# A decoder trunk on one NeuronCore: its opening written in another order, with the first norm folded

## The chip, the cores and the metric

The kernel runs on one core of one Trainium2 chip. Its time is the device time of one launch in microseconds (us): 993.72 us is the median of three runs (992.82 to 994.13). One execution was profiled; it took 992.12 us, of which its span, from the first instruction to the last, is 990.1 us. In what follows PE is TensorE, PEld its weight loads, DVE is VectorE, ACT is ScalarE, POOL is GpSimd and SP is SyncE, which here only issues transfers.

## The reference

A trunk of two layers over 1024 positions of 1024 channels, f32. Only the first sub-layer matters here:

```
c_act = silu(c)
shift, scale, gate = split(c_act @ ada_w[0] + ada_b[0], 3)
h = (x * rsqrt(mean(x*x, -1) + eps) * norm_g[0]) * (1 + scale) + shift
u, z = split(h @ a_w_in, 2);  p = causal_multiscale_pool(u)      # four groups of 512 channels
y = grouped(p) @ a_w_group * a_scale;  x = x + gate * ((y * silu(z)) @ a_w_out)
```

After it come a shared K/V, a sliding-window attention layer with sinks, and a final norm. In group 0 the kernel multiplies the input weight by the group weight first ("joined" weight), so that the pooled product needs one matmul chain less.

## The kernel before, in words

Channels lie on partitions, positions on the free axis; position halves of 512 are called q = 0 and 1, and the eight blocks of 128 channels k = 0 to 7. A float32 product is made of three passes in the faster fp32r format: each operand is split in a rounded part "h" and a rest "l" (`h` by ACT, `l = raw - h` by DVE or POOL), and h*h, h*l and l*h are summed in PSUM.

The opening, which ends at the first matmul of the gates (L218), is a list of calls (L424 to L550) under a manual schedule: on each of the five engines the instructions stand in just the order in which they are written, and each engine takes them in that order. What it does:

- SP issues loads in the order of L425 to L434: four chunks `ci` of the two weights to be joined (`wgr`, `raw`, 0.25 and 0.5 MiB), the halves of `x` (0.25 MiB each), then the scale tiles `ad` (two of 0.5 MiB for each k, L294). The buffers of `raw` and of `ad` are two each, so later loads wait until the earlier content is used.
- `split_wg` and `split_wu` (L299, L304) split a chunk; `join_mm` (L312) makes 96 matmuls of 512 columns, 8 output blocks by 4 chunks by 3 passes; `joined_h` and `joined_l` split the joined weight w0 again (for blocks 2, 3, 6 and 7 ACT copies it and POOL subtracts, L329 and L336).
- c, one row, is spread to 128 partitions by a matmul with ones (L459, here as two fp32r passes of `crow`), then silu is made of it (`cact`, L468 and L470).
- `square2` and `add2` (L407, L416) make the sum of squares of x over the eight blocks, `rstd_stats` (L136) sums it over partitions with 1-column matmuls and takes the power -0.5 on POOL, `rstd_spread` (L154) spreads it to a tile `rbs[q]`.
- `dots(k, i)` (L342) gives shift (i = 0) and scale (i = 1) of block k: a DVE product-and-sum over 1024 columns (L247), after which `mod_scale` (L266) makes the column `acol`.
- For each k and q, `first_xn` (DVE, x times rstd, L181), `first_h` (ACT makes h, L163, and again the same in f32, L378; POOL makes l, L379), and `first_mm` (12 matmuls, L402) with w0. For k = 0 the f32 value and l are made by DVE (`soon_h`, `soon_l`).

`first_mm` runs for k = 0, 4, 1, 5, 2, 6, 3, 7. After the opening `block_sums` (L607) forms sums and differences of the modulated blocks for the gates' and inputs' products. From there on the instructions keep the order that the kernel before has.

Of the kernel before, what the change touches and what calls it, by code (L numbers as in the profile page):

```python
# [49 lines left out]
CONST_FILL = 56  # L50
# [5 lines left out]
def trunk(ctx, tc, xT, c, pack, ada_first, ada_rest, wu0_in, wg0_in, wa, wg, wao, wkv,  # L56
# [57 lines left out]
    acol = cp.tile([P, 24], F32, name="acol")  # L114
# [107 lines left out]
    with ExitStack() as sa:  # L222
# [19 lines left out]
        crow = hp.tile([P, 2, T], F32R, tag="h", name="crow")  # L242
        onesr = sp.tile([P, H], F32R, tag="xn", name="onesr", bufs=5)[:, :P]
        nc.vector.tensor_copy(out=onesr[0:1, :], in_=ones[0:1, :].broadcast_to([1, P]))

# [81 lines left out]
        copies = {}  # L327

        def joined_raw(*ms):  # L329

            for m in ms:
                if m % 2 == 0:
                    copies[m // 2] = tmp()
                nc.scalar.copy(out=copies[m // 2][:, half(m % 2)], in_=jb[m])

        def joined_sub(*ms):  # L336
            for m in ms:
                w = w0[m // 2][:, m % 2]
                nc.gpsimd.tensor_sub(out=w[:, 1, :], in0=copies[m // 2][:, half(m % 2)],
                                     in1=w[:, 0, :].bitcast(F32))  # L340
# [6 lines left out]
        xns = {}  # L347

        def first_xn(k, q):
            xns[k, q] = xn_tile(k, q, rbs[q])  # L350
# [30 lines left out]
        def soon_h(k, q):  # L381
            a, b, h, _ = first_parts(k, q)
            mod_h(xns[k, q], a, b, h)
            nc.vector.tensor_scalar(out=first_f(k, q), in0=xns[k, q], scalar1=a, scalar2=b,
                                    op0=ALU.mult, op1=ALU.add)

        def soon_l(k, q):
            _, _, h, l = first_parts(k, q)
            nc.vector.tensor_sub(out=l, in0=first_f(k, q), in1=h.bitcast(F32))
# [14 lines left out]

        sqs = {}

        def square2(n, q):  # L407

            if n < 2:
                sqs[n, q] = sq2[q][n]  # L410
            elif n % 2 == 0:
                t = tmp()
                sqs[n, q], sqs[n + 1, q] = t[:, half(0)], t[:, half(1)]
            nc.scalar.activation(sqs[n, q], xk[n][:, half(q)], AF.Square)

        def add2(n, q, eng=None):  # L416
            s = sq2[q][n % 2]
            (eng or nc.vector).tensor_add(out=s, in0=s, in1=sqs[n, q])

        def fold(q):  # L420
            nc.vector.tensor_add(out=sq2[q][0], in0=sq2[q][0], in1=sq2[q][1])

        ET = mybir.EngineType
        with tc.manual_schedule(engines={ET.PE, ET.Activation, ET.DVE, ET.Pool, ET.SP}):  # L424
            fetch_c(0, (half(0), half(1)))  # L425
            nc.sync.dma_start(pk, pack)
            fetch_c(1)
            fetch_x(0, range(4))
            fetch_c(2)
            fetch_c(3)  # L430
            fetch_x(0, range(4, 8))
            fetch_x(1, range(8))
            fetch_ada(0)
# [11 lines left out]

            warm(5)
# [3 lines left out]
            for cols in (half(0), half(1)):  # L450
                split_wu(0, cols)
            nc.vector.tensor_copy(out=crow[0:1, 0, :], in_=cact[0:1, :])
            nc.vector.tensor_sub(out=crow[0:1, 1, :], in0=cact[0:1, :],
                                 in1=crow[0:1, 0, :].bitcast(F32))
            for i in range(3):
                join_all(0, s=(i,))
            for q in range(2):
                for i in range(2):
                    mm(cbs[q], onesr[0:1, :], crow[0:1, i, half(q)], start=i == 0, stop=i == 1)  # L459
# [7 lines left out]
            for q in range(2):  # L467
                nc.scalar.activation(cact[:, half(q)], cbs[q], AF.Tanh, scale=0.5)  # L468
            for q in range(2):
                nc.vector.scalar_tensor_tensor(out=cact[:, half(q)], in0=cact[:, half(q)],  # L470
                                               scalar=1.0, in1=cbs[q], op0=ALU.add, op1=ALU.mult)
            split_wg(2)
            split_wu(2)
            join_all(2)
            split_wg(3)
            split_wu(3)
            nc.vector.tensor_scalar_mul(out=asch, in0=pk[:, C_ASC:C_ASC + 16], scalar1=0.5)
            nc.vector.tensor_scalar_mul(out=nsink, in0=pk[:, C_SINK:C_SINK + 16], scalar1=-1.0)
            for k in range(4, 8):
                square2(k, 0)  # L480
                add2(k, 0)
            fold(0)
            for k in range(3):
                square2(k, 1)
            join_all(3, (4, 5))
            rs = rstd_stats(sq2[0][0], 4)
            joined_h(4, 5)
            joined_l(4, 5)
            square2(3, 1)
            join_all(3, (0,))  # L490
            add2(2, 1)
            add2(3, 1, nc.gpsimd)
            square2(4, 1)
            joined_h(0)
            join_all(3, (1,))
            bc = rstd_spread(rs, 4)
            square2(5, 1)
            joined_l(0)
            joined_h(1)
            add2(4, 1)  # L500
            add2(5, 1, nc.gpsimd)
            nc.scalar.copy(out=rbs[0], in_=bc)
            join_all(3, (2, 3))
            square2(6, 1)
            joined_l(1)
            square2(7, 1)
            dots(0, 0)
            add2(6, 1, nc.gpsimd)
            joined_h(2, 3)
            joined_raw(2, 3)  # L510
            dots(0, 1)
            add2(7, 1)
            fold(1)
            joined_sub(2)
# [3 lines left out]
            for ci in range(3):  # L518
                join_mm(7, jb[7], ci)
            first_xn(0, 0)  # L520
            soon_h(0, 0)
            rs = rstd_stats(sq2[1][0], 4)
            soon_l(0, 0)
            joined_h(6)
            joined_raw(6)
            joined_sub(3)
            dots(4, 0)
            dots(4, 1)
            join_mm(7, jb[7], 3)
            bc = rstd_spread(rs, 4)  # L530
            first_mm(0, 0)
# [920 lines left out]
```

## Time and profile before

| | |
|---|---|
| median of three runs | 993.72 us |
| the profiled execution | 992.12 us |
| its span | 990.1 us |
| PE busy | 964.8 us (97%), 4530 instructions |
| DVE busy | 783.8 us (79%) |
| ACT busy | 467.7 us (47%) |
| POOL busy | 179.2 us (18%) |
| moved by DMA | 125.67 MB, mean 127 GB/s |

A span of 97% busy PE says little on the opening, which is 9% of it: there the tables of stretches and the timeline are read. "Idle before" in brackets is how long the engine stood still ahead of an instruction, and what it waited for. A matmul of 512 columns shows as 0.39 us though the next starts some 0.23 us later, since they overlap in the pipeline; DVE and ACT instructions overlap by 0.07 to 0.1 us in the same way.

### The profile page before, as it was taken

The numbers are of one execution on the slowest core, as the hardware profiler recorded it, in microseconds if no ns is written. First come the engines' busy times: TensorE is split into PE (matmuls) and PEld (weight loads), VectorE is DVE, ScalarE is ACT, GpSimd is POOL, SyncE is SP. The second block draws the span as 40 slices with busy tenths as digits, with TensorE's granted clock in tenths as the row PEclk, the third lists the DMA queues.
The fourth block names the chain that finished last, engine by engine and source line by source line (L and its number), as shares of the span: only waits on it lengthen the run. The fifth ranks groups of instructions, "written<-read, shape, count | busy, mean of one in ns | idle before, by whom it ended". The sixth has DMA issues, their size and how long they took to land.

```text
span 990.1 us, 12704 instructions
## 1 busy us (share of the span) xinstructions
PE 964.8 (97%) x4530; PEld 799.8 (81%) x4530; DVE 783.8 (79%) x1405; ACT 467.7 (47%) x912; POOL 179.2 (18%) x194
## 2 busy tenths in 40 slices
PE   8899999999999999999999998999999999999996
PEld 7677888888888887888888886877788888887786
DVE  6998977776987699676782268599899877889985
ACT  7445434433443344551111135486777555656544
POOL 3652000000000000000000000043334212335723
PEclk9999999999999999999999999999999999999998
DMA  9462532164216411779861213312222221123222
GB/s 325 153 205 107 178 107 78 50 226 149 64 66 211 149 64 47 263 275 338 303 219 43 86 47 96 135 53 75 71 73 71 86 87 64 65 86 107 86 86 85
DMA packets 40625, 125.67 MB, mean 127 GB/s; under 512 B 4465, under 2 KB 6641, under 8 KB 40434
## 3 DMA queue, kind: packets, MB, share of 16 engines
q1 hardware_dynamic: 40416, 123.82, 37.0%
q10 hardware_dynamic: 146, 1.05, 0.3%
q8 instruction: 35, 0.57, 0.2%
q14 instruction: 28, 0.23, 0.1%
HBM read 111.22 MB, written 13.63 MB: 126 GB/s over the span
## 4 chain that ended last, share of the span: by engine, by line
PE 71%; DVE 21%; ACT 4%; issue 2%; POOL 1%; DMA 0%; POOLq 0%; DVEq 0%; SPq 0%; ACTq 0%
PE ps_d L218 13%; PE ps_d L663 9%; PE ps_S L218 8%; PE ps_d L207 5%; PE ps_d L209 5%; PE ps_d L208 5%; PE ps_S L663 4%; PE ps_o L218 4%; PE ps_tp L218 3%; DVE wl L123 3%; PE ps_o L663 2%; PE ps_tp L663 2%; PE ps_d L402 2%; DVE tmp L578 2%; DVE ad L247 1%
## 5 line engine op out<-in xcount | busy, mean ns | idle before, releaser
L121 ACT CAST wh<-raw 128x1024 fp32r<-128x1024 f32 x80 | 83.7, 1047 | 108.2 <-PE ps_d L218 84.0
L123 DVE TENSOR_TENSOR wl<-raw,wh 128x1024 fp32r<-128x1024 f32 x80 | 103.0, 1287 | 39.8 <-ACT wh L121 36.0
L207 PE MATMUL ps_d<-hm,wh 128*128 128x512 f32 x288 | 113.9, 396 | 1.1 <-ACT wh L121 1.1
L209 PE MATMUL ps_d<-hm,wl 128*128 128x512 f32 x288 | 112.7, 391 | 1.4 <-DVE wl L123 1.4
L208 PE MATMUL ps_d<-hm,wh 128*128 128x512 f32 x288 | 112.4, 390 | 0.0
L218 PE MATMUL ps_d<-gh,wh 128*128 128x512 f32 x224 | 82.0, 389 | 0.0
L247 DVE CUSTOM_DVE_ANT_0 tmp<-tmp,cact,pk 128x1024 f32<-128x1024 f32 x48 | 60.8, 1283 | 26.0 <-DMA tmp<-ada_rest 25.8
L209 PEld LDWEIGHTS ps_d<-hm,wl 128*128 128x128 f32 x288 | 54.1, 188 | 14.4 <-DVE wl L123 3.0
L218 PE MATMUL ps_S<-gh,wh 128*128 128x512 f32 x192 | 64.6, 390 | 0.0
L207 PEld LDWEIGHTS ps_d<-hm,wh 128*128 128x128 f32 x288 | 54.1, 188 | 11.7 <-ACT wh L121 1.7
L663 PE MATMUL ps_d<-hs,ws 128*128 128x512 f32 x264 | 63.4, 389 | 0.0
L1135 ACT ACTIVATE pt<-pt,nm 128x129 f32<-128x129 f32 x128 | 50.1, 394 | 26.6 <-DVE nm L1131 24.3
L208 PEld LDWEIGHTS ps_d<-hm,wh 128*128 128x128 f32 x288 | 54.2, 188 | 9.8
L663 PEld LDWEIGHTS ps_d<-hs,ws 128*128 128x128 f32 x264 | 49.6, 188 | 10.3
L570 POOL MEMSET tmp<- 128x16 f32 x16 | 1.7, 112 | 288.1 <-DVE adac L247 122.2
L639 ACT CAST ws<-tw 128x512 fp32r<-128x512 f32 x44 | 26.7, 622 | 54.6 <-PE ps_tp L218 15.1
L663 PE MATMUL ps_d<-ha,ws 128*128 128x512 f32 x216 | 51.9, 389 | 0.0
L578 DVE TENSOR_TENSOR tmp<-tmp 128x1039 f32<-128x1039 f32 (+3 forms) x40 | 49.4, 1235 | 1.9 <-ACT tmp L699 0.9
L151 POOL TENSOR_TENSOR rs<-v,mhalf 128x4 f32<-128x4 f32 (+1 forms) x7 | 6.6, 940 | 235.9 <-DVE v L146 216.7
L218 PEld LDWEIGHTS ps_d<-gh,wh 128*128 128x128 f32 x224 | 42.1, 188 | 8.7
L663 PEld LDWEIGHTS ps_d<-ha,ws 128*128 128x128 f32 x216 | 40.5, 188 | 8.4
L218 PE MATMUL ps_d<-gh,wl 128*128 128x512 f32 x112 | 43.6, 389 | 0.0
(301 smaller groups left out, 2530.5 us busy)
## 6 DMA issues: line engine op xcount, KB each, us to landing
tmp<-ada_rest SPq DMA_DIRECT2D x48, 512.0 KB, 4.3
raw<-wb SPq DMA_DIRECT2D x32, 512.0 KB, 3.3
raw<-wa SPq DMA_DIRECT2D x28, 512.0 KB, 3.5
raw<-wao SPq DMA_DIRECT2D x20, 512.0 KB, 3.9
x<-xT SPq DMA_DIRECT2D x32, 256.0 KB, 6.1
ad<-ada_first SPq DMA_DIRECT2D x16, 512.0 KB, 4.6
raw<-wbo SPq DMA_DIRECT2D x16, 512.0 KB, 3.3
kept_g<-tmp SPq DMA_DIRECT2D x14, 512.0 KB, 2.9
```

The lines of the kernel that those rows point to most:

```text
L121: nc.scalar.copy(out=wh, in_=raw)
L123: nc.vector.tensor_sub(out=wl, in0=raw, in1=wh.bitcast(F32))
L207: mm(ps, lh, acts(k, 0), start=k == 0, stop=False)
L208: mm(ps, lh, acts(k, 1), start=False, stop=False)
L209: mm(ps, ll, acts(k, 0), start=False, stop=k == n - 1)
L218: mm(p, lhs, acts(k, hl, q), start=start and k == 0 and s == 0, stop=stop and k == n - 1 and s == 2)
L247: nc.vector.tensor_tensor_reduce(out=raw, in0=raw, in1=ca, scale=0.5, scalar=pk[:, bcol:bcol + 1], op0=ALU.mult, op1=ALU.add, accum_out=ad ...
L402: mm(psu[i, q], w0[k // 2][:, k % 2, w, i * P:(i + 1) * P], block(k, q)[hl], start=k == 0 and s == 0, stop=k == KT - 1 and s == 2)
L578: nc.vector.tensor_add(out=nx[:, 2 * s - 1:], in0=cur[:, 2 * s - 1:], in1=cur[:, s - 1:PAD + T - s])
L639: nc.scalar.copy(out=ws[i][:, 0, :], in_=src)
L663: mm(ps, lhs, acts(k, hl), start=start and k == 0 and s == 0, stop=k == 3 and s == 2, skip_group_check=True)
L1135: nc.scalar.activation(pt[:, i, :P + 1], pt[:, i, :P + 1], AF.Exp, bias=nm[:, i:i + 1], scale=-1.0, accum_out=den[:, i:i + 1])
```

## The change

The list of the opening is written anew. SP loads the scale tiles of block 0 second, right behind chunk 0 and `pack`, and the second four blocks of x ahead of chunk 3. The spread of c stands ahead of the joins as two plain f32 matmuls, without `crow`. `dots(0, ..)` stand behind the split of chunk 1; `acol` is made by ACT in place of DVE. In the second half of positions the two partial sums of squares are no more added on DVE: `rstd_stats` sums both in PSUM. All additions of squares are on DVE, all `joined_l` too. `first_h` is now a DVE product x*a*rstd in place (L351 of the changed kernel) and one ACT addition of the shift (L353); `first_l` (L357) makes l on DVE as (x + shift) - h. x then lacks the shift, so `block_sums` adds it back. POOL is left with the splits of the chunks and the powers.

```
 def rstd_stats(sq, n, more=None):
-        def sums(t, c0):
+        for i, t in enumerate((sq,) if more is None else (sq, more)):
             for j in range(n):
-                mm(st[:, c0 + j:c0 + j + 1], t[:, j * P:(j + 1) * P], invd, start=True, stop=True)
+                mm(st[:, j:j + 1], t[:, j * P:(j + 1) * P], invd, start=i == 0 and j == 0,
+                   stop=j == n - 1 and (i == 1 or more is None))
-        sums(sq, 0)
         nc.vector.tensor_scalar_add(out=v[:, :n], in0=st[:, :n], scalar1=EPS)
-        if more is not None:
-            sums(more, n)
-            nc.vector.tensor_add(out=v[:, :n], in0=st[:, n:2 * n], in1=v[:, :n])
...
         def dots(k, i):
             ada_dot(ads[k][i], cact, 8 * i + k, C_ADAB + 8 * i + k)
             if i:
-                mod_scale(k, 8 + k, C_NG + k, 1)
+                g = pk[:, C_NG + k:C_NG + k + 1]
+                nc.scalar.activation(acol[:, k:k + 1], adac[:, 8 + k:9 + k], AF.Identity,
+                                     bias=g, scale=g)
...
         def first_h(k, q):
-            a, b, h, l = first_parts(k, q)
-            mod_h(xns[k, q], a, b, h)
-            nc.scalar.activation(first_f(k, q), xns[k, q], AF.Identity, bias=b, scale=a)
-            nc.gpsimd.tensor_sub(out=l, in0=first_f(k, q), in1=h.bitcast(F32))
+            a, b, h, _ = first_parts(k, q)
+            nc.vector.scalar_tensor_tensor(out=first_f(k, q), in0=first_f(k, q), scalar=a,
+                                           in1=rbs[q], op0=ALU.mult, op1=ALU.mult)
+            nc.scalar.activation(h, first_f(k, q), AF.Identity, bias=b, scale=1.0)
+        def first_l(k, q):
+            _, b, h, l = first_parts(k, q)
+            nc.vector.scalar_tensor_tensor(out=l, in0=first_f(k, q), scalar=b,
+                                           in1=h.bitcast(F32), op0=ALU.add, op1=ALU.subtract)
...
             fetch_c(0, (half(0), half(1)))
             nc.sync.dma_start(pk, pack)
+            fetch_ada(0)
             fetch_c(1)
             fetch_x(0, range(4))
             fetch_c(2)
+            fetch_x(0, range(4, 8))
             fetch_c(3)
-            fetch_x(0, range(4, 8))
             fetch_x(1, range(8))
-            fetch_ada(0)
             fetch_ada(4)
...
+            for q in range(2):
+                mm(cbs[q], ones[0:1, :].broadcast_to([1, P]), cact[0:1, half(q)],
+                   start=True, stop=True)
             split_wg(0)
...
             split_wg(1)
             split_wu(1)
-            for k in range(4):
-                square2(k, 0)
-            for k in range(2, 4):
-                add2(k, 0)
+            dots(0, 0)
+            dots(0, 1)
             join_all(1)
+            squares(0, 0, 1, 2, 3)
+            adds(0, 2, 3)
             split_wg(2)
             split_wu(2)
             join_all(2)
+            squares(0, 4, 5, 6, 7)
+            adds(0, 4, 5, 6, 7)
             split_wg(3)
             split_wu(3)
+            squares(1, 0, 1)
+            rs = rstd_stats(fold(0), 4)
...
+            rs = rstd_stats(sq2[1][0], 4, sq2[1][1])
+            dots(4, 0)
+            joined_h(6)
+            joined_l(6)
+            for ci in range(4):
+                join_mm(7, jb[7], ci)
+            bc = rstd_spread(rs, 4)
+            nc.scalar.copy(out=rbs[1], in_=bc)
+            joined_h(7)
+            joined_l(7)
+            first_mm(0, 0)
+            first_h(0, 1)
+            dots(4, 1)
+            first_l(0, 1)
             first_mm(0, 1)
...
                 for q in range(2):
-                    first_xn(k, q)
+                    if k != 4:
+                        first_l(late[0], q)
+                        first_mm(late[0], q)
                     first_h(k, q)
-                    first_mm(k, q)
+                late[0] = k
...
+            parts = ((0, f22, f21, bs, f22, add, add), (2, f21, f11, None, f21, None, sub),
+                     (1, f11, f22, b1, f11, sub, sub), (3, f12, f12, b2, f11, add, sub))
```

On ACT the place is from the split of chunk 0 to that of chunk 2; `wgs` and `wu` are the split weights, `first` and `tmp` the squares of x, `cact` the silu of c. Before:

```order
L308 CAST wu<-raw 128x512 x2
L300 CAST wgs<-wgr 128x512
L308 CAST wu<-raw 128x1024
L414 ACTIVATE first<-x 128x512 x2
L414 ACTIVATE tmp<-x 128x512 x2
L468 ACTIVATE cact<-ps_tp 128x512
L468 ACTIVATE cact<-ps_o 128x512
L300 CAST wgs<-wgr 128x512
L308 CAST wu<-raw 128x1024
```

The same place in the changed kernel:

```order
L300 CAST wu<-raw 128x512
L420 ACTIVATE cact<-ps_tp 128x512
L300 CAST wu<-raw 128x512
L420 ACTIVATE cact<-ps_o 128x512
L292 CAST wgs<-wgr 128x512
L300 CAST wu<-raw 128x1024
L323 ACTIVATE acol<-adac,pk 128x1
L385 ACTIVATE first<-x 128x512 x2
L385 ACTIVATE tmp<-x 128x512 x2
L292 CAST wgs<-wgr 128x512
L300 CAST wu<-raw 128x1024
```

The silu of c has moved ahead of chunk 1, and between the casts of chunk 1 and the squares stands the one-column `acol`, which needs the second of DVE's two products (`ISA`, L239) for block 0.

On DVE the place is one round of the repeated part, from the products of one block k to those of the next (`ISA` is the product and the reading of its sum). Before:

```order
L247 ISA ad,adac<-ad,cact,pk 128x1024
L247 ISA adac 128x1
L247 ISA ad,adac<-ad,cact,pk 128x1024
L247 ISA adac 128x1
L266 SCALAR_TENSOR_TENSOR acol<-adac,pk 128x1
L181 TENSOR_TENSOR xn<-x,second 128x512 x2
```

The same round in the changed kernel:

```order
L239 ISA ad,adac<-ad,cact,pk 128x1024
L239 ISA adac 128x1
L239 ISA ad,adac<-ad,cact,pk 128x1024
L239 ISA adac 128x1
L357 SCALAR_TENSOR_TENSOR ha<-x,adac,ha 128x512
L351 SCALAR_TENSOR_TENSOR x<-x,acol,second 128x512
L357 SCALAR_TENSOR_TENSOR a_484<-x,adac,a_484 128x512
L351 SCALAR_TENSOR_TENSOR x<-x,acol,second 128x512
```

DVE has two more instructions of 512 columns in a round and no one-column instruction; L357 belongs to the block before, L351 to the block whose products stand above it.

## Rows read from the trace of the kernel before

**Rows 1.** Busy time, share of the span and instructions of each engine.

```profile
PE 964.8 (97%) x4530; PEld 799.8 (81%) x4530; DVE 783.8 (79%) x1405; ACT 467.7 (47%) x912; POOL 179.2 (18%) x194
```

**Rows 2.** Stretches: length, busy PE, PEld, DVE, ACT, POOL, clock, DMA share, GB/s.

```profile
5.00:10.00 5.00, 4.92 (x14) 3.95 (x15) 3.60 (x5) 2.36 (x5) 2.19 (x2) 1.00 0.97 331
10.00:15.00 5.00, 5.00 (x22) 3.58 (x21) 3.98 (x6) 4.97 (x9) 1.30 (x1) 1.00 1.01 361
...
35.00:40.00 5.00, 4.45 (x19) 3.69 (x19) 4.83 (x8) 2.06 (x4) 4.49 (x3) 0.66 0.32 107
...
57.00:63.00 6.00, 6.00 (x26) 4.54 (x25) 5.97 (x9) 3.12 (x5) 3.48 (x2) 1.00 0.84 291
...
87.00:110.00 23.00, 23.00 (x103) 19.06 (x102) 22.01 (x33) 9.89 (x17) 0.22 (x2) 1.00 0.57 198
```

**Rows 3.** Chain that ended last, 0 to 110 us: start, length, what.

```profile
22.09 0.80 PE ps_o L142 x8
...
51.55 3.32 PE ps_d L402 x12
...
86.65 0.23 PE ps_d L218
```

**Rows 4.** Timeline, 1 to 25 us: start, length, engine, line, what.

```profile
1.92 2.50 PE L440 MATMUL ps_S<-ident 128*128 128x128 f32 x10 [1.92 <-POOL ident masks.py:199]
...
2.66 0.20 ACT L110 ACTIVATE early<-ones 128x1 f32<-128x1 f32 x1
...
8.91 1.05 ACT L308 CAST wu<-raw 128x1024 fp32r<-128x1024 f32 x1 [0.69 <-DMA raw<-wu]
...
9.86 1.15 ACT L414 ACTIVATE first<-x 128x512 f32<-128x512 f32 x2
9.99 1.22 DVE L309 TENSOR_TENSOR wu<-raw,wu 128x1024 fp32r<-128x1024 f32 x1 [1.26 <-ACT wu L308]
...
11.72 0.62 PE L459 MATMUL ps_o<-crow,onesr 1*128 1x512 f32 x2
...
16.48 2.88 PE L315 MATMUL ps_d<-wgs,wu 128*128 128x512 f32 x12
...
19.20 2.88 PE L315 MATMUL ps_S<-wgs,wu 128*128 128x512 f32 x12
...
20.90 0.69 DVE L421 TENSOR_TENSOR first<-first 128x512 f32<-128x512 f32 x1
...
22.99 1.28 DVE L325 TENSOR_TENSOR w<-ps_S,w 128x512 fp32r<-128x512 f32 x2
...
23.15 1.02 POOL L151 TENSOR_TENSOR rs<-v,mhalf 128x4 f32<-128x4 f32 x1 [5.94 <-DVE v L146]
...
24.23 1.16 PE L158 MATMUL ps_tp<-ident,rs 128*128 128x128 f32 x8
```

**Rows 5.** Timeline, 26 to 60 us, columns as in rows 4.

```profile
26.50 1.19 DVE L418 TENSOR_TENSOR second<-second,tmp 128x512 f32<-128x512 f32 x1
...
34.21 1.02 PE L142 MATMUL ps_o<-invd,second 128*128 128x1 f32 x8 [2.65 <-DVE second L421]
...
51.16 1.28 DVE L247 CUSTOM_DVE_ANT_0 ad<-ad,cact,pk 128x1024 f32<-128x1024 f32 x1
...
52.28 1.32 POOL L379 TENSOR_TENSOR ha<-x,ha 128x512 fp32r<-128x512 f32 x1 [3.52 <-ACT x L378]
...
52.37 2.31 DVE L247 CUSTOM_DVE_ANT_0 ad<-ad,cact,pk 128x1024 f32<-128x1024 f32 x1
...
54.72 1.13 DVE L266 SCALAR_TENSOR_TENSOR acol<-adac,pk 128x1 f32<-128x1 f32 x1
...
56.98 1.27 DVE L247 CUSTOM_DVE_ANT_0 ad<-ad,cact,pk 128x1024 f32<-128x1024 f32 x1
```

**Rows 6.** Durations by line, ns: least, median, most; first and last start.

```profile
L919 DVE SCALAR_TENSOR_TENSOR tmp<-x,acol,rb x16: 743/744/748, 578.9 to 613.3; 128x512 f32<-128x512 f32 x16
...
L921 ACT ACTIVATE hm<-tmp,adac x16: 723/725/727, 579.7 to 614.1; 128x512 fp32r<-128x512 f32 x16
```

More of the change, by code (lines that the diff above doesn't have):

```diff
@@ L48 @@
 ENDS = (0, 1, 3, 5, 7)
-CONST_FILL = 56
+CONST_FILL = 44
 SLOT_FILL = 32
@@ L325, in joined_l @@
                 nc.vector.tensor_sub(out=w[:, 1, :], in0=jb[m], in1=w[:, 0, :].bitcast(F32))
[L327 to L340, printed above, removed]
         def dots(k, i):
@@ L403, in first_mm, with squares, adds @@
                    start=k == 0 and s == 0, stop=k == KT - 1 and s == 2)
+        sq2 = [[t[:, 1, half(i)] for i in range(2)] for t in (first_t, second_t)]
         sqs = {}
[L407 to L418, printed above, removed]
+        def squares(q, *ks):
+            for n in ks:
+                if n < 2:
+                    sqs[n, q] = sq2[q][n]
+                elif n % 2 == 0:
+                    t = tmp()
+                    sqs[n, q], sqs[n + 1, q] = t[:, half(0)], t[:, half(1)]
+                nc.scalar.activation(sqs[n, q], xk[n][:, half(q)], AF.Square)
+        def adds(q, *ks):
+            for n in ks:
+                s = sq2[q][n % 2]
+                nc.vector.tensor_add(out=s, in0=s, in1=sqs[n, q])
         def fold(q):
             nc.vector.tensor_add(out=sq2[q][0], in0=sq2[q][0], in1=sq2[q][1])
+            return sq2[q][0]
         ET = mybir.EngineType
@@ L444, in join_all, with c_tanh, c_act @@
                     join_mm(m, jb[m], ci, s)
+            def c_tanh(q):
+                nc.scalar.activation(cact[:, half(q)], cbs[q], AF.Tanh, scale=0.5)
+            def c_act(q):
+                nc.vector.scalar_tensor_tensor(out=cact[:, half(q)], in0=cact[:, half(q)],
+                                               scalar=1.0, in1=cbs[q], op0=ALU.add, op1=ALU.mult)
             warm(5)
@@ L448, in trunk @@
             cbs = [bank(t) for t in ("tp", "o")]
+            for q in range(2):
+                mm(cbs[q], ones[0:1, :].broadcast_to([1, P]), cact[0:1, half(q)],
+                   start=True, stop=True)
             split_wg(0)
[L450 to L454, printed above, removed]
+            split_wu(0, half(0))
+            c_tanh(0)
+            split_wu(0, half(1))
+            c_tanh(1)
+            c_act(0)
+            c_act(1)
             for i in range(3):
                 join_all(0, s=(i,))
-            for q in range(2):
-                for i in range(2):
-                    mm(cbs[q], onesr[0:1, :], crow[0:1, i, half(q)], start=i == 0, stop=i == 1)
             split_wg(1)
             split_wu(1)
-            for k in range(4):
-                square2(k, 0)
-            for k in range(2, 4):
-                add2(k, 0)
+            dots(0, 0)
+            dots(0, 1)
             join_all(1)
[L467 to L471, printed above, removed]
+            squares(0, 0, 1, 2, 3)
+            adds(0, 2, 3)
             split_wg(2)
@@ L474, in trunk @@
             join_all(2)
+            nc.vector.tensor_scalar_mul(out=asch, in0=pk[:, C_ASC:C_ASC + 16], scalar1=0.5)
+            nc.vector.tensor_scalar_mul(out=nsink, in0=pk[:, C_SINK:C_SINK + 16], scalar1=-1.0)
+            squares(0, 4, 5, 6, 7)
+            adds(0, 4, 5, 6, 7)
             split_wg(3)
             split_wu(3)
[L477 to L484, printed above, removed]
+            squares(1, 0, 1)
+            rs = rstd_stats(fold(0), 4)
             join_all(3, (4, 5))
-            rs = rstd_stats(sq2[0][0], 4)
             joined_h(4, 5)
+            squares(1, 2, 3)
+            adds(1, 2, 3)
             joined_l(4, 5)
-            square2(3, 1)
             join_all(3, (0,))
-            add2(2, 1)
-            add2(3, 1, nc.gpsimd)
-            square2(4, 1)
+            bc = rstd_spread(rs, 4)
+            nc.scalar.copy(out=rbs[0], in_=bc)
             joined_h(0)
-            join_all(3, (1,))
-            bc = rstd_spread(rs, 4)
-            square2(5, 1)
+            squares(1, 4)
+            join_all(3, (1, 2, 3))
+            first_h(0, 0)
+            adds(1, 4)
             joined_l(0)
             joined_h(1)
[L500 to L504, printed above, removed]
-            joined_l(1)
[L506 to L514, printed above, removed]
+            squares(1, 5, 6)
+            adds(1, 5, 6)
+            joined_l(1)
+            joined_h(2)
+            squares(1, 7)
+            adds(1, 7)
             jb += [bank("S") for _ in range(2)]
@@ L547, in trunk @@
                 for q in range(2):
-                    first_xn(k, q)
+                    if k != 4:
+                        first_l(late[0], q)
+                        first_mm(late[0], q)
                     first_h(k, q)
-                    first_mm(k, q)
+                late[0] = k
+            for q in range(2):
+                first_l(7, q)
+                first_mm(7, q)
         traced = nc.cur_bb.bb.instructions
```

59 lines of the change are left out of this document (19 added, 40 removed).

## The prediction

> **What bounds the kernel now.** The page comes first: PE is busy for 97% of the span [rows 1], so there is little left to win except where PE stands still. The table of stretches tells where that is. From 87 us on PE has no idle time (23.00 of 23 us), and DVE only just keeps up with it (22.01) [rows 2]. So whatever the opening gains or loses, up to the first matmul of the gates at 86.65 us [rows 3], is passed on to the end of the kernel undiminished, and the forecast is the shift of that one point. The chain of waits gives two more marks [rows 3]: the sums of squares of the first half start on PE at 22.09, and block k = 1, where the repeated part begins, at 51.55. That divides the opening into a front (22.09 us, ruled by loads and splits), a middle (29.46 us) and six repeated rounds (35.10 us).
>
> In the front the transfers run at full share, at 331 to 361 GB/s [rows 2], and the cast of chunk 1 waits for its load at 8.91 [rows 4]. In the rounds DVE is busy 5.97 of 6 us [rows 2], and the timeline shows why [rows 5]: the first product of a round takes 1.28 us, the second, while POOL subtracts, 2.31, and the one-column instruction behind it 1.13; from one round to the next, 51.16 to 56.98, it is 5.82 us. PE's own work in a round is 24 matmuls. Twelve of them start in 19.20 - 16.48 = 2.72 us where nothing waits [rows 4], so a round is 5.44 us of PE.
>
> **The rounds.** POOL's subtraction and ACT's second f32 pass go, DVE's `xn` and `acol` go; DVE gets four instructions with a column operand, of the kind that takes 0.744 us [rows 6], one every 0.67 since neighbours overlap by some 0.07. With POOL still, both products cost 1.25: 2.5 + 4 x 0.67 = 5.2 us, under PE's 5.44. What is late next is PE itself. h is made a round ahead and l in time for the last four of twelve matmuls, so I cost nothing there; the cover is 0.24 us in a round. The six rounds then take 144 x 0.2267 = 32.6 us, against 35.1: **-2.5 us**. The bounds are 0 (DVE stays as slow as now) and -2.5 (PE can't go faster).
>
> **The front.** SP issues two more tiles of 0.5 MiB, 1.05 MB, ahead of chunk 1; everything behind them in SP's queue lands later by 1.05 MB / 331 to 361 GB/s, 2.9 to 3.2 us; I take 3.0. Then along the engines, with the durations of rows 4 (ACT 0.55 for a square or cast of 512 columns, two being 1.15; DVE 0.6 for one of 512, two being 1.28):
> - the cast of chunk 1 starts at 11.9 and ends at 12.95; DVE's rest (1.22) ends at 14.2, the two products of block 0 (2.5) at 16.7, ACT's `acol` (0.20 for such a column) at 16.95;
> - in ACT's queue behind `acol` stand four squares and both casts of chunk 2. So ACT, which has nothing else, waits from 12.95 to 16.7. Four squares (2.2), the `wgs` cast (0.55) and the `wu` cast (1.05) end at 20.75, the rest on DVE at 22.05;
> - chunk 2's matmuls need that rest from the third pass on: 16 x 0.2267 more, PE done at 25.7. They started at 16.48 before;
> - DVE: two small ones (0.15), four additions (2.4), the rest of chunk 3 (1.22; its cast is done at 24.55), the fold (0.69): 26.5. POOL's rest of `wgs` falls on this stretch twice. An addition beside POOL took 1.19 [rows 5], one without 0.69 [rows 4], so +0.5 for one of the two.
>
> The sums of squares thus start at 27.0 in place of 22.09: **+4.9 us**. The ends: 24.0 if the early tiles delayed nothing (+1.9), 28.0 if both POOL instructions cost 0.5 and the transfers 3.2 plus a share of the wait for chunk 3 (+5.9). I take 27.0, as the load of chunk 1 is seen to be waited for.
>
> The Trainium skill (SBUF — State Buffer, "Who interferes with whom") has a DVE instruction with two SBUF inputs and a GpSimd instruction that reads SBUF lock each other out until the first is finished. Here that would make an addition wait up to POOL's 1.3 us rather than 0.5, and the front 0.8 longer; rows 5 show 1.19 against 0.69, so I keep 0.5.
>
> The c spread: five warm-up matmuls of 128 f32 columns take 2.50 us [rows 4], 0.5 each, so 512 f32 columns are between 0.31 (what the fp32r pair's 0.62 is each) and 2.0 us; I take 2.0. Two end at 8.4 us, and chunk 0's 18 matmuls (4.1 us) at 12.5. PE waits for chunk 1's rest until 14.2 anyway: no cost. Without that cover, at most 4.0 - 0.6 = 3.4.
>
> **The middle**, from the start of the sums (t = 0), with the same durations, 0.80 for four of PE's column sums [rows 3], 1.02 for the power, and 0.9 for a spread, whose 1.16 overlaps the next matmul by 0.25 [rows 4]:
> - PE: sums 0.8, six joins 2.15, three 2.85, spread 3.75, nine joins 5.8, block 6 (12 joins) 8.5;
> - ACT copies two joined blocks (3.4), then squares 2 and 3 (4.5); DVE adds them (5.2), two rests (6.4), h of block 0 (7.1), an addition and a rest (8.3); ACT's h, copy and squares 5 and 6 end at 9.5, DVE's additions at 10.2, a rest and the last addition at 11.4;
> - so PE waits: the second sums end at 12.25, block 7 at 15.0, spread 15.9, (0,0) 18.6. ACT's copies of the spread and of joined block 7 (17.1), DVE's rest (17.75) and h (18.4) and ACT's h (19.2) stand ahead of (0,1), which ends at 21.95;
> - (4,0) runs eight matmuls to 23.75 and waits for its l, which DVE has behind a product, l, two h, and two products: 24.95. (4,1) ends at 28.6.
>
> 28.6 against 29.46: **-0.9 us**. PE's own work in it is 24.6 us, the lower bound; the upper is the 29.46 of now.
>
> **The sum.** 27.0 + 28.6 + 32.6 = 88.2 against 86.65: +1.6 us (+4.9 - 0.9 - 2.5, rounded). The rest is nothing: `block_sums` gets 12 instructions 0.05 us longer (0.744 of [rows 6] for 0.69 of [rows 4]) and a small one of 0.15, 0.8 us of DVE, under PE that has no gap [rows 2]; without that cover it is 0.8. The final norm's sums lose one DVE instruction a quarter, which stood beside PE's second sums. The profiled execution took 992.12 (span 990.1 and 2.0 around it); it would be 993.7. That execution lies 1.6 under the median 993.72, so on the median's scale I forecast **995.3 us**. Some 0.2% (2.0 us) is what a measurement of this kernel can tell from no change, and +1.6 lies within.
>
> **Rivals.**
> - *PE's clock falls in the front* (slower, +3.3). PE is done with chunk 1 at 14.2 + 16 x 0.2267 = 17.85 and starts chunk 2 at 20.75, 2.9 us of rest. Before, PE stood still for 2.65 us ahead of 34.21 [rows 5], and the granted clock from 35 to 40 was 0.66 [rows 2], a loss of 5 x 0.34 = 1.7 us. If that falls on chunk 2, its end moves from 25.7 to 27.4 or, all at the lower of the two levels, 1.2 GHz, to 29.3; it decides from 27.0 on. I take 28.7, +1.7 on the sum. Against: half of it is hidden by the fold. The skill (TensorE: Matmul & The Clock Gate, "What's actually happening") says the engine is throttled by default and activity releases it; what row 35 to 40 shows agrees, and by that rule this rival is the forecast.
> - *DVE stays the bound in the rounds* (slower, +4.1): if the products stay near 2.3 without POOL, the rounds take 35.1. For: the second product was 2.31 in every round. Against: the first, without POOL, was 1.28.
> - *The middle runs at PE's pace* (faster, -2.4 to -3.9): 24.6 us in place of 28.6, since POOL disturbs nothing there; with half of the transfers' delay hidden, 1.5 less again. I price it at -2.9. For: DVE's stretched work in the middle goes. Against: the waits above are between ACT and DVE, not POOL's.
>
> **How the numbers follow.** The forecast gets 0.62; its own range is -0.5 to +3.2, of which 0.40 under 2.0 us and 0.22 above. The clock 0.13, DVE bound 0.07, both slower. The middle at PE's pace 0.18: 0.14 faster, 0.04 within. Sums: faster 0.14, within 0.2% 0.44, slower 0.42. The range reaches from -1.1, short of the faster case, to +3.9, past the clock and just short of the dearest rival: 992.6 to 997.6.
>
> **What would show it.** Right: ACT idle some 3.7 us ahead of the squares, released by DVE's sum; the second-half marks at 27, 55.6 and 88.2; products of 1.28 throughout; rounds of 5.44 with PE never idle. Wrong: chunk 1's cast before 11 us (the transfer term), a low clock between 20 and 28 (the first rival), rounds near 5.8 (the second), block k = 1 reached before 53 (the third).

## The result, and the profile after

The changed kernel takes 996.83 us (median of six runs, 996.06 to 998.71), the kernel before in runs beside it 993.45 (six runs, 992.71 to 994.23): ratio 1.0036, 95% interval 1.0023 to 1.0049, so 3.4 us slower. Forecast were 995.3 in a range of 992.6 to 997.6, with no change that can be told as the likeliest class; what came is inside the range and is a slowdown that can be told. The profiled execution took 996.06, the shortest of the six and 3.9 more than the one of before; its span is 994.4.

PE's busy time is 4.8 us longer with eight instructions more: of it 2.6 are the spread of c, two matmuls of 2.07 and 1.91 us in place of two pairs of 0.73 and 0.62, and most of the rest fits the low clock that the stretches below show. DVE, ACT and POOL have less to do than in [rows 1]:

```profile
PE 969.6 (98%) x4538; PEld 805.2 (81%) x4538; DVE 775.1 (78%) x1411; ACT 458.0 (46%) x902; POOL 144.3 (15%) x173
```

The table of stretches of the changed kernel, columns as in [rows 2]:

```profile
20.00:25.00 5.00, 3.69 (x10) 2.58 (x11) 4.32 (x7) 5.00 (x9) 2.54 (x2) 0.81 1.05 408
25.00:30.00 5.00, 5.00 (x23) 3.99 (x23) 2.80 (x5) 0.70 (x2) 0.98 (x1) 0.85 0.93 379
...
35.00:40.00 5.00, 3.71 (x25) 3.04 (x24) 4.41 (x8) 3.82 (x8) 0.00 (x0) 1.00 0.01 3
40.00:45.00 5.00, 5.00 (x19) 4.07 (x19) 2.59 (x6) 0.00 (x0) 2.09 (x3) 0.66 0.32 105
...
57.00:63.00 6.00, 6.00 (x28) 4.99 (x27) 6.00 (x11) 1.84 (x3) 0.00 (x0) 1.00 0.72 249
...
87.00:110.00 23.00, 23.00 (x103) 19.05 (x102) 19.94 (x29) 9.20 (x15) 0.22 (x2) 1.00 0.43 150
```

Read the clock column, third from the end: it is below 1.00 from 20 to 30 and from 40 to 45, where before it fell once, from 35 to 40. From 57 on PE is busy without a gap. DVE's 19.94 in the last row (22.01 before) is not a gain: its work there comes 4 us later than before, and counted from the gates on, from 91.03 to 114.03, DVE is busy for 22.31 of 23 us. The chain of waits, columns as in [rows 3]:

```profile
16.76 0.39 ACT acol L323
...
22.30 3.98 PE ps_d L307 x10
...
27.83 0.91 PE ps_o L142 x8
...
38.91 1.05 PE ps_o L142 x8
39.97 4.44 PE ps_S L307 x12
...
58.04 2.72 PE ps_d L371 x12
...
63.48 2.72 PE ps_d L371 x12
...
90.68 0.23 PE ps_d L214
```

The three marks: the sums start at 27.83 (22.09 before), block k = 1 at 58.04 (51.55), the first matmul of the gates at 90.68 (86.65). So the front is 5.74 us longer, the middle 0.75 longer (30.21), the rounds 2.46 shorter (32.64, six of 5.44): together 4.03. Behind the last mark both kernels take the same, 994.4 - 90.68 = 903.7 and 990.1 - 86.65 = 903.5. The timeline, columns as in [rows 4]:

```profile
4.36 2.07 PE L430 MATMUL ps_tp<-cact,ones 1*128 1x512 f32 x2
...
12.01 1.05 ACT L300 CAST wu<-raw 128x1024 fp32r<-128x1024 f32 x1 [0.63 <-DMA raw<-wu]
...
14.23 1.28 DVE L239 CUSTOM_DVE_ANT_0 ad<-ad,cact,pk 128x1024 f32<-128x1024 f32 x1
...
16.76 0.39 ACT L323 ACTIVATE acol<-adac,pk 128x1 f32<-128x1 f32 x1 [3.70 <-DVE adac L239]
...
20.73 0.98 PE L307 MATMUL ps_d<-wgs,wu 128*128 128x512 f32 x2 [1.97 <-ACT wu L300]
...
22.32 3.58 DVE L390 TENSOR_TENSOR first<-first,tmp 128x512 f32<-128x512 f32 x4
...
23.36 1.38 POOL L293 TENSOR_TENSOR wgs<-wgr,wgs 128x512 fp32r<-128x512 f32 x1 [2.21 <-ACT wgs L292]
...
26.96 0.68 DVE L393 TENSOR_TENSOR first<-first 128x512 f32<-128x512 f32 x1
...
37.81 2.16 PE L142 MATMUL ps_o<-invd,second 128*128 128x1 f32 x16 [1.21 <-DVE second L390]
...
39.83 4.58 PE L307 MATMUL ps_S<-wgs,wu 128*128 128x512 f32 x12
...
40.87 1.99 POOL L147 TENSOR_TENSOR rs<-v,mhalf 128x4 f32<-128x4 f32 x1 [10.82 <-DVE v L145]
```

ACT stands still for 3.70 us ahead of `acol`, and everything in its queue is late by that. The four additions at 22.32, one of them beside POOL, take 3.58. The row at 39.83 is the one to compare: block 7's twelve matmuls take 4.58 us where twelve took 2.88 in [rows 4]. Beside them POOL's power, while DVE runs a product, takes 1.99 us where it took 1.02 in [rows 4].

### The profile page after: what moved, and what is told of

It is laid out like the page before. It is cut to its first block, busy times and chain, and to the rows that moved or that the text cites. A ratio compares the mean times of both kernels' runs of the same rounds, so it can differ in the third digit from the quotient of the medians.

```text
span 994.4 us, 12698 instructions
## 1 busy us (share of the span) xinstructions
PE 969.6 (98%) x4538; PEld 805.2 (81%) x4538; DVE 775.1 (78%) x1411; ACT 458.0 (46%) x902; POOL 144.3 (15%) x173
## 4 chain that ended last, share of the span: by engine, by line
PE 73%; DVE 17%; ACT 4%; issue 2%; DMA 2%; POOL 1%; SPq 0%; POOLq 0%; DVEq 0%; ACTq 0%
PE ps_d L214 13%; PE ps_d L639 9%; PE ps_S L214 8%; PE ps_d L203 6%; PE ps_d L205 6%; PE ps_d L204 6%; PE ps_S L639 4%; PE ps_o L214 4%; PE ps_tp L214 3%; DVE wl L123 3%; PE ps_o L639 2%; PE ps_tp L639 2%; DVE tmp L545 2%; PE ps_d L371 2%; ACT wh L121 1%
## 5 line engine op out<-in xcount | busy, mean ns | idle before, releaser
L239 DVE CUSTOM_DVE_ANT_0 tmp<-tmp,cact,pk 128x1024 f32<-128x1024 f32 x48 | 60.7, 1282 | 28.9 <-DMA tmp<-ada_rest 28.8
L205 PEld LDWEIGHTS ps_d<-hm,wl 128*128 128x128 f32 x288 | 54.1, 188 | 14.5 <-DVE wl L123 3.0
L1111 ACT ACTIVATE pt<-pt,nm 128x129 f32<-128x129 f32 x128 | 50.1, 394 | 26.8 <-DVE nm L1107 24.6
```

The lines of the kernel that those rows point to most:

```text
L205: mm(ps, ll, acts(k, 0), start=False, stop=k == n - 1)
L239: nc.vector.tensor_tensor_reduce(out=raw, in0=raw, in1=ca, scale=0.5, scalar=pk[:, bcol:bcol + 1], op0=ALU.mult, op1=ALU.add, accum_out=ad ...
L1111: nc.scalar.activation(pt[:, i, :P + 1], pt[:, i, :P + 1], AF.Exp, bias=nm[:, i:i + 1], scale=-1.0, accum_out=den[:, i:i + 1])
```

## The experiments

Ten kernels ran, each beside the kernel before (993.1 to 993.3 there). The table has the three stretches by the chain of each trace; the ratio is to the kernel before. In the run with the load order the chain goes over a transfer at the first mark, so it is taken from the timeline (22.48, which counts 0.14 less than a chain does). A trace is of one execution, which can lie off the median of its run: 998.22 for 996.31 with fillers in the middle and 988.07 for 986.57 with c as a pair, each the longest of five. The loads vary too: with the scale tiles loaded second, the cast of chunk 1 started between 11.01 and 13.23 us in the six traces that have this order of loads (12.01 in the changed kernel's), and all of the front shifts with it.

| run | front | middle | rounds | median us | ratio (95%) |
|---|---|---|---|---|---|
| before | 22.09 | 29.46 | 35.10 | 993.45 | |
| changed | 27.83 | 30.21 | 32.64 | 996.83 | 1.0036 (1.0023-1.0049) |
| fillers in the middle | 29.39 | 30.10 | 32.64 | 996.31 | 1.0035 (1.0023-1.0047) |
| `acol` late | 24.62 | 30.37 | 32.64 | 993.89 | 1.0010 (1.0001-1.0018) |
| load order | 22.6 | 31.5 | 32.64 | 992.35 | 0.9991 (0.9982-1.0000) |
| rounds alone | 22.62 | 30.28 | 32.64 | 991.76 | 0.9986 (0.9978-0.9995) |
| fillers in the front | 28.16 | 30.33 | 32.64 | 995.66 | 1.0028 (1.0016-1.0039) |
| sums apart | 29.23 | 29.44 | 32.64 | 996.49 | 1.0030 (1.0018-1.0042) |
| reordered | 22.10 | 25.05 | 32.64 | 985.89 | 0.9927 (0.9914-0.9939) |
| reordered, sums in a row | 22.71 | 25.04 | 32.64 | 985.05 | 0.9920 (0.9907-0.9934) |
| reordered, c as a pair | 23.25 | 26.44 | 32.64 | 986.57 | 0.9933 (0.9920-0.9945) |
| reordered, front as changed | 29.79 | 25.03 | 32.64 | 991.05 | 0.9981 (0.9972-0.9990) |

**Fillers in the middle.**

```diff
+            def fill(n, tag):
+                ps = bank(tag)
+                for _ in range(n):
+                    mm(ps, wus[0][:, 0, :P], wgs[0][:, 0, :], start=True, stop=True)
...
+            fill(5, "o")
             rs = rstd_stats(sq2[1][0], 4, sq2[1][1])
```

> The changed kernel with five extra matmuls (a product of chunk 0 into a bank that nobody reads) on PE in front of the second half's sums of squares, where PE stood idle for 1.21 us at 36.6 to 37.8. Theory A (the clock is what the middle lost): PE rests for 1.21 us and then runs sixteen one-column sums, the granted clock falls to 0.66 from 40 to 45, and block 7's twelve matmuls take 4.44 us in place of 2.72. With the rest filled the clock stays at 1.00 there, block 7 takes 2.7, block k = 1 comes at 56.3 in place of 58.04, and the time falls by 1.7 us, from 996.8 to 995.1. Rival B (the middle is set by ACT and DVE between the spread and the second quarter, so a faster block 7 only waits longer): block k = 1 stays within 0.4 us of 58.04, no change of time. Rival C (the one-column sums themselves bring the clock down): block 7 stays at 4.4 and the time is the same or up to 0.3 us longer.

Timeline of this run:

```profile
37.89 1.29 PE L418 MATMUL ps_o<-wgs,wu 128*128 128x512 f32 x5
39.26 2.16 PE L142 MATMUL ps_o<-invd,second 128*128 128x1 f32 x16
41.28 4.58 PE L307 MATMUL ps_S<-wgs,wu 128*128 128x512 f32 x12
```

Theory A fell: most of the idle time is filled and block 7 still takes 4.58. What a middle at the full clock would have gained was thus not measured by this run. In this execution the front's low clock also lasted longer: chunk 2's sixteen matmuls took 6.58 us by the chain (5.53 in the changed kernel's trace), and the sums started at 29.39.

**`acol` late.**

```diff
-            if i:
...
+            if i and k:
+                acol_col(k)
+
+        def acol_col(k):
+            g = pk[:, C_NG + k:C_NG + k + 1]
...
             squares(1, 0, 1)
             rs = rstd_stats(fold(0), 4)
+            acol_col(0)
```

> The changed kernel with block 0's one-column activation (acol) moved down ACT's queue, from ahead of the first four squares to behind the first two squares of the second half; the scale tiles are still loaded second. It tells ACT's wait from the transfer. Theory A (most of the front's 5.7 us is ACT standing still from 13.06 to 16.76 for the products): ACT goes on with the squares at about 13.1, the cast of chunk 2 follows its load at about 16.7 in place of 19.6, chunk 2's matmuls follow chunk 1's without a rest, and the first sums start at about 24.3 in place of 27.8, -3.5 us; the time falls to about 993.3. Theory B (the 1.05 MB of transfers alone set it): the sums stay at 27 or later and the time is within 1 us of 996.8.

Its timeline:

```profile
11.01 1.04 ACT L300 CAST wu<-raw 128x1024 fp32r<-128x1024 f32 x1 [0.67 <-DMA raw<-wu]
11.96 1.15 ACT L388 ACTIVATE first<-x 128x512 f32<-128x512 f32 x2
...
24.62 1.05 PE L142 MATMUL ps_o<-invd,first 128*128 128x1 f32 x8 [1.28 <-DVE first L396]
```

Theory A holds: ACT goes on with the squares as soon as chunk 1 is cast, PE doesn't rest ahead of chunk 2, and the front is 3.2 us shorter. Of that 1.0 is not `acol`'s: the load of chunk 1, which this edit doesn't touch, landed earlier in this execution (cast at 11.01 for 12.01). From that cast to the sums it is 13.61 us for 15.82. So one column instruction of 0.39 us, placed ahead of four squares, cost 2.2 us by the traces, and 2.9 by the medians (993.89 for 996.83), in which the front's low clock has a part too (below). Taking the transfers out as well (next run) brings the sums 2.0 earlier than here.

**Load order.**

```diff
-            fetch_ada(0)
             fetch_c(1)
...
             fetch_x(1, range(8))
+            fetch_ada(0)
             fetch_ada(4)
...
-            dots(0, 0)
-            dots(0, 1)
             join_all(1)
...
             rs = rstd_stats(fold(0), 4)
+            dots(0, 0)
+            dots(0, 1)
...
             joined_h(0)
+            acol_col(0)
```

> The changed kernel with block 0's scale tiles loaded where the kernel before loads them (behind all of x), the two products of block 0 behind the first sums of squares, and its acol behind the copy of joined block 0. It takes away both the transfer and ACT's wait; the c spread stays first and in f32. Theory: chunk 1 is there at 9 to 10 us, but PE's chunk 0 ends only at 14.5, because the spread's two f32 matmuls take 4.0 us at the low clock, and this cover is now gone; then chunks 1 and 2 take 8.2 us without a rest, so the sums start at about 23 in place of 27.8 (22.09 before). The time falls by 4 to 5 us, to about 992. Rival (the c spread costs nothing here either): the sums start at 22.1 or earlier. Rival (the later products collide with DVE's work in the middle): the sums start at 23 but block k = 1 at 55 or later, a gain of 3 or less.

Its timeline:

```profile
14.32 2.88 PE L307 MATMUL ps_d<-wgs,wu 128*128 128x512 f32 x12
...
15.82 2.49 DVE L393 TENSOR_TENSOR first<-first,tmp 128x512 f32<-128x512 f32 x4
...
22.48 0.95 PE L142 MATMUL ps_o<-invd,first 128*128 128x1 f32 x8
...
29.49 3.02 PE L307 MATMUL ps_S<-wgs,wu 128*128 128x512 f32 x12 [0.91 <-DVE w L317]
```

As expected: chunk 1 starts at 14.32, when the spread and chunk 0 let it, the sums at 22.5, and the time is 992.35. A part is given back in the middle (31.5), where PE now waits 0.91 for a rest that DVE has behind the two products. The same four additions take 2.49 here, with POOL still until 18.14, against 3.58 in the changed kernel.

**Rounds alone.** The kernel before with `first_h`, `first_l`, `acol` on ACT, the loop and `block_sums` of the changed one:

```diff
-            first_xn(0, 0)
-            soon_h(0, 0)
+            first_h(0, 0)
...
                 for q in range(2):
-                    first_xn(k, q)
+                    if k != 4:
+                        first_l(late[0], q)
+                        first_mm(late[0], q)
                     first_h(k, q)
-                    first_mm(k, q)
```

> The kernel before with the folded first norm alone (products with a column operand on DVE, no GpSimd subtraction, sums of blocks with the shift added, acol on ACT); its load order, its c spread and the written order of its opening stay. Theory: the first sums start at 22.1 as before, block k = 1 near 51.5 or somewhat earlier, since (4,0) and (4,1) no longer wait for POOL, and a round takes 5.44 in place of 5.82 to 5.9: the first matmul of the gates comes at about 84, -2.5 us, and the time is about 990.9. Rival (l made a round late takes from the middle what the rounds gain): 993, no change.

Its stretches:

```profile
35.00:40.00 5.00, 4.46 (x22) 3.78 (x22) 4.37 (x6) 1.68 (x3) 3.90 (x3) 0.65 0.31 113
40.00:45.00 5.00, 5.00 (x17) 3.94 (x16) 3.28 (x6) 3.26 (x6) 2.66 (x2) 0.67 0.41 151
```

The rounds give their 2.46 us, the three stretches together 1.1 and the medians 1.5: the front came 0.5 later (chunk 1 was cast at 9.89, in the kernel before at 8.91, with the same order of loads), and the middle is 0.8 longer, with the low clock over two rows where the kernel before has one.

**Fillers in the front.**

```diff
             join_all(1)
...
+            fill(12, "o")
             join_all(2)
```

> The changed kernel with twelve extra matmuls (a product of chunk 0 into a bank that nobody reads) on PE between chunk 1 and chunk 2, where PE rested 1.97 us and the granted clock from 20 to 30 us was 0.81 and 0.85. Theory A (the low clock is seen in the front, but DVE hides it): the clock stays at 1.00, chunk 2's last sixteen matmuls take 3.6 us in place of 5.5 and end at about 26, but the fold on DVE ends at 27.64 as before, so the sums start at 27.7 in place of 27.83 and the time stays within 0.5 us of 996.8. Theory B (the clock is the front's loss): the sums start at 26 to 26.5, and the time falls by 1.5 us or more.

Its timeline:

```profile
25.07 1.52 PE L307 MATMUL ps_S<-wgs,wu 128*128 128x512 f32 x6
...
28.16 1.02 PE L142 MATMUL ps_o<-invd,first 128*128 128x1 f32 x8 [1.57 <-DVE first L393]
```

The clock stays at 1.00, chunk 2 is done at 26.6, and PE waits 1.57 us for the fold. The cast of chunk 1 started 0.33 later here (12.34), and so did the sums: from that cast it is 15.82 us to them in both kernels. So in the trace of the changed kernel the front's low clock was hidden. The median is 1.2 lower all the same, though the intervals overlap. That fits other traces with the changed front, where the low clock held until PE was the later of the two: in three of them (fillers in the middle, sums apart, front as changed) it is 16.56 to 16.88 us from the cast to the sums, 0.7 to 1.1 more. Which share of the executions that is isn't traced; the changed kernel's trace is of its shortest.

**Sums apart.** `join7(a, b)` makes joins a to b of block 7's twelve; the last argument is called between the two tiles' sums.

```diff
-            rs = rstd_stats(sq2[1][0], 4, sq2[1][1])
...
+            join7(0, 4)
+            rs = rstd_stats(sq2[1][0], 4, sq2[1][1], lambda: join7(4, 7))
...
-            for ci in range(4):
-                join_mm(7, jb[7], ci)
+            join7(7, 12)
```

> The changed kernel with the second half's sixteen one-column sums taken apart on PE: four joins of block 7, the sums of the first tile, three joins, the sums of the second tile, five joins; no matmul more or less. The run with five fillers ahead of the sums kept block 7 at 4.45 us, so it is the sums in a row (2.16 us), not the idle time, that is now suspected. Theory A (sums in a row act as a rest): with joins between them the granted clock from 38 to 45 stays at 1.00, the twelve joins take 2.7 us in all, the spread comes at about 42.3 in place of 44.41, block k = 1 at about 56 in place of 58.04, and the time falls by 2 us, to 994.8. Rival B (any sums bring the low clock): the spread still comes earlier by the 0.9 us that the four joins fill, but the rest runs at the low clock: block k = 1 at 57, -1 us. Rival C (ACT and DVE set the middle): block k = 1 within 0.4 us of 58.04.

Its timeline:

```profile
39.10 1.02 PE L144 MATMUL ps_o<-invd,second 128*128 128x1 f32 x8 [0.30 <-DVE second L392]
...
40.76 0.95 PE L144 MATMUL ps_o<-invd,second 128*128 128x1 f32 x8
41.56 2.15 PE L309 MATMUL ps_S<-wgs,wu 128*128 128x512 f32 x5
44.20 1.71 PE L156 MATMUL ps_tp<-ident,rs 128*128 128x128 f32 x8 [0.49 <-POOL tmp L545]
```

Rival B, roughly: the middle is 0.8 shorter, and the last five joins still take 2.15 us. The spread then waits 0.49 us for POOL, whose power takes 1.99 us here as in the changed kernel. The median is 0.3 under the changed kernel's, within the scatter.

**Reordered.** Load order and `acol` as in the runs above, and a new list for the middle:

```diff
-            squares(1, 0, 1)
-            rs = rstd_stats(fold(0), 4)
+            squares(1, 0, 1, 2, 3, 4, 5, 6, 7)
+            sq = fold(0)
+            adds(1, 2, 3)
+            rs = rstd_stats(sq, 4)
...
+            join_all(3, (1,))
+            joined_h(1)
+            rs = rstd_stats(sq2[1][0], 4, sq2[1][1], lambda: join_all(3, (2,)))
...
+            join_all(3, (3,))
...
             for ci in range(4):
                 join_mm(6, jb[6], ci)
...
+            bc = rstd_spread(rs, 4)
...
             for ci in range(4):
                 join_mm(7, jb[7], ci)
...
             first_mm(0, 0)
...
             first_mm(0, 1)
```

> All findings in one: the changed kernel with the load order of before, block 0's products behind the first sums and its acol out of ACT's way, and besides a new order in the middle: ACT squares all of the second half before it copies joined blocks, the second sums stand in two groups among chunk 3's joins, and blocks 6 and 7 come behind them, with the spread between. Theory: the first sums start at 22.5 as in the run with the load order; behind them PE has 24.6 us of work and nothing to wait for, so block k = 1 comes at 47 to 48 in place of 51.55 before and 58.04 now; with rounds of 5.44 the first matmul of the gates comes at about 80 and the time is about 986, -7 us against before. Rival (DVE, with 22 us of work in this stretch, and the later scale tiles set the middle): block k = 1 at 50 or later, -3 to -4 us, about 990.

Its chain:

```profile
22.10 0.79 PE ps_o L144 x8
...
29.87 2.75 PE ps_S L309 x12
...
33.51 2.76 PE ps_S L309 x12
...
47.15 2.72 PE ps_d L376 x12
...
79.79 0.23 PE ps_d L216
```

Right in each mark: 22.10, 47.15, 79.79, and 985.89 us. The chain is PE alone from 20 us to the gates, the clock 1.00 in every stretch from 10 to 87. This beats both kernels: 7.4 us (0.73%) under the one before.

**Reordered, sums in a row.**

```diff
-            rs = rstd_stats(sq2[1][0], 4, sq2[1][1], lambda: join_all(3, (2,)))
+            rs = rstd_stats(sq2[1][0], 4, sq2[1][1])
+            join_all(3, (2,))
```

> The reordered kernel with the second half's sixteen one-column sums again in a row on PE, in front of chunk 3's joins for block 2 in place of around them; nothing else moves, and PE has no idle time before or behind. In the run with the sums apart the five joins behind them still went at the low clock, but PE had also waited there (0.30 us before, 0.49 behind), so the cause is open. Theory A (sums in a row are enough to bring the low clock): behind the sums, from 28.5 on, the granted clock falls to 0.66 over some 5 us as in the changed kernel, the joins there lose 1.7 us, block k = 1 comes at 48.9 in place of 47.15, and the time is about 987.6 in place of 985.9. Theory B (it takes the sums and idle time together): the clock stays at 1.00, 985.9.

Its timeline:

```profile
27.13 1.84 PE L144 MATMUL ps_o<-invd,second 128*128 128x1 f32 x16
28.84 1.65 PE L309 MATMUL ps_d<-wgs,wu 128*128 128x512 f32 x6
```

Theory B: sixteen sums in a row take 1.84 us, the joins behind them go at the full clock, and the time is no longer (985.05; the intervals overlap). The sums alone didn't bring the clock down here.

**Reordered, c as a pair.** The c spread of the kernel before (`crow`, four short matmuls behind chunk 0), with the silu of c behind the casts of chunk 2, and:

```diff
-            rs = rstd_stats(sq, 4)
             join_all(3, (4, 5))
+            rs = rstd_stats(sq, 4)
```

> The reordered kernel with the c spread of before: c split into two fp32r rows on DVE and spread by four short matmuls behind chunk 0, where the changed kernel spreads it by two f32 matmuls (4.0 us) ahead of chunk 0; the first sums stand behind chunk 3's joins of blocks 4 and 5, since their squares aren't ready earlier. Theory A (with the transfers out of the way the f32 spread is no longer covered): chunk 0 starts at 5.1 in place of 8.06, chunk 1 at 12.3 in place of 13.78, and the 1.5 us reach block k = 1, 45.7 in place of 47.15: about 984.4. Theory B (loads and DVE, which has no idle time from 25 us on, take them back): 47.15 and 985.9, so the f32 spread costs nothing even here.

Its timeline:

```profile
12.34 3.02 PE L312 MATMUL ps_d<-wgs,wu 128*128 128x512 f32 x12
...
22.03 1.21 PE L312 MATMUL ps_S<-wgs,wu 128*128 128x512 f32 x4 [0.78 <-DVE wu L306]
...
25.77 1.96 PE L156 MATMUL ps_tp<-ident,rs 128*128 128x128 f32 x8 [0.94 <-POOL rs L149]
```

Chunk 1 does start 1.4 us earlier, but PE then waits 0.78 for DVE's rest and 0.94 for the power, and the granted clock from 25 to 30 is 0.66. Block k = 1 comes at 49.69 in this execution, for 47.15; the front and the middle don't compare singly, as the first sums stand six joins later. By the medians the two kernels are the same within their intervals. So in this order the pair gains nothing over the f32 spread; an order in which its 1.4 us would be kept wasn't tried.

**Reordered, front as changed.** The scale tiles are loaded second again, and `acol` stands right behind the products, in front of the squares:

```diff
             nc.sync.dma_start(pk, pack)
+            fetch_ada(0)
             fetch_c(1)
...
             split_wu(1)
+            dots(0, 0)
+            dots(0, 1)
```

> The reordered kernel with the front of the changed kernel put back as it was: block 0's scale tiles loaded second, its products and acol ahead of the first squares. So only the front is that of the changed kernel, and the middle has no waits that could take up or add anything. Theory A (the front's delay is passed on whole): the first sums start at 27.8 to 29.3 in place of 22.10, the middle keeps its 25.05 us, block k = 1 comes at 53 to 54.3, and the time is 5.7 to 7.2 us longer than the reordered kernel's 985.9: 991.6 to 993.1. Rival (the middle takes part of it up, since the two products are then done before it): +3 to +4.5, 989 to 990.5.

PE's rest ahead of chunk 2, and its chain:

```profile
21.96 1.27 PE L309 MATMUL ps_d<-wgs,wu 128*128 128x512 f32 x2 [2.45 <-ACT wu L302]
...
23.52 4.64 PE ps_d L309 x10
28.16 1.63 PE ps_S L309 x6
29.79 0.79 PE ps_o L144 x8
...
54.82 2.72 PE ps_d L373 x12
```

Theory A by the trace (the middle keeps its 25.03 behind a front of 29.79) and just under its lower end by the median: +5.2 us. Here chunk 2 ran at the low clock but for its end, so that its last 16 matmuls took 6.27 us in place of 3.63; chunk 1 was cast at 13.23, the latest of the six traces.

## Why the forecast was right or wrong

- **The rounds** were right: 5.44 each, products of 1.28 as forecast, PE never idle; -2.46 for -2.5. The second rival is out.
- **The front** was right in its mechanism and 0.8 short: +5.74 for +4.9. The transfer (cast of chunk 1 at 12.01 for 11.9), the products and ACT's wait (3.70 for 3.7) came as worked out, the transfer with some luck, as other executions had that cast at 11.01 to 13.23; `acol` took 0.39 for 0.20. The mis-sized term is POOL's: I took 0.5 for the two POOL subtractions together. The additions took 3.58 against 2.49 with POOL still (load order), 1.1 more, and chunk 2's rest 1.53 against 1.22, 0.3 more: 1.4 for 0.5, the whole of the miss, as other terms were a little shorter. The Trainium skill (SBUF — State Buffer, "Who interferes with whom") has these two kinds of instruction exclude each other; by its rule the forecast gave 27.8 for the sums, and the trace has 27.83.
- **The middle** failed at the term "block 7 at 15.0" from the start of the sums. The second sums ended at 12.14 (39.97 - 27.83) as forecast (12.25), but the twelve joins behind them, sized at 2.72, took 4.44 at the granted clock of 0.66. On the chain that 1.72 stands for the whole miss, 30.21 for 28.6, the rest of the stretch being 0.1 shorter. A second term was too small behind it: the power, put at 1.02, took 1.99 and ended at 42.86, so with joins of 2.72 the spread could have come some 1.5 us earlier than its 44.41, and not 1.72. No run took the low clock alone out of this middle, so its price there is read from the chain and not shown by a run. I had priced a low clock, at 1.7, only for the front; [rows 2, 5] showed one at just this place in the kernel before, behind a rest and the second sums, and my new middle kept a rest and sums there.
- **The first rival** was right on the clock in the front (0.81 and 0.85) and in the traced execution wrong on the price, since the fold hid it; in three other traces of this front 0.7 to 1.1 of the 1.7 was paid.
- **The third rival**, the middle at PE's pace, did not come (30.21 for 24.6). The reason given against it was right: the waits were between ACT and DVE. With the new list of the reordered kernel, squares ahead of the copies of joined blocks and the second sums among chunk 3's joins, the middle took 25.05.
- **The c spread** was right at no cost: 2.07 and 1.91 us a matmul for the 2.0 taken, and the pair is no faster in the one order tried without that cover. Chunk 0's 18 matmuls took 6.4 us rather than 4.1 and ended at some 14.5 rather than 12.5, just as chunk 1's rest came: they start 0.43 us apart up to 12.5 and 0.23 apart behind, though the granted clock is 1.00 from 5 to 15. What was late by that, the rest of PE ahead of chunk 2 took up.
- **The tail** was right: 0.2 us.

So +1.6 was forecast on the traced execution and +3.9 came: 0.8 from POOL beside DVE, 1.7 at block 7, less 0.1. That the time still lies inside the range owes something to luck: the room above 995.3 was kept for a low clock in the front, and it was filled by one in the middle and by POOL. The new order of the opening costs what the folded norm earns and more: alone the fold is worth 1.5 us, and the changed front 5.2.

## What to carry to other kernels

On an engine that works in written order, look at what stands behind an instruction that waits for another engine: moving one small column instruction out of ACT's way gave back 2.9 us by the medians without touching a transfer. Price a rest of PE with the matmuls behind it as well, at the clock that the trace grants after such rests, and at each place where the new order still has one. Before a saving in one trace is put down to an edit, look whether the loads landed at the same time in both. The list in which PE never waits kept the full clock and beat both kernels.

## What the runs showed of the hardware

- Sixteen one-column sums took 1.84 us where their data were ready, and the clock stayed at 1.00 (reordered, sums in a row). In the run with fillers in the middle the same sixteen took 2.16, since DVE's last addition was not done, and the clock fell to 0.50, the lower of the two levels, about a microsecond behind them. So in the middle it fell behind sums that had waits among them and not behind sums alone; in the front it fell behind a rest of 1.97 us without sums. What of it brings the fall stays open.
- How long the low clock lasts differs between traces of the same front: in the changed kernel it lay between about 23 and 26.5 us, in three other kernels with that front from about 21.5 to 28.5. PE had rested 1.97 us ahead of chunk 2 in the first and 2.42 to 2.45 in the three, so a longer rest may be the cause; no run varies the rest alone.
- Loads in the same order landed at different times: the cast of chunk 1 started from 11.01 to 13.23 us over six traces.
- POOL's power (128 by 4) took 1.99 us beside a product on DVE and 1.02 with DVE idle (at 29.02 in the changed kernel).
- A column activation on ACT (128 by 1, both operands columns) took 0.39 us, twice the 0.20 of the one in [rows 4].
